# Unsplit 32-bit attention matmuls in place of three-part splits, in a two-layer encoder trunk

## The chip, the core and the metric

The kernel runs on one core of one Trainium2 chip. The metric is the device time of one execution in microseconds (us). The engines are TensorE (PE; its weight loads are listed as PEld), VectorE (DVE), ScalarE (ACT), GpSimd (POOL) and SyncE (SP, which here only issues transfers).

## What is computed

Two layers, each over 512 prompt frames and 32 sample frames, with 1024 features, all in 32-bit floats. A layer is a feed-forward block, a mixer, a second feed-forward block and a gated input embedding, each between two norms. The mixer is where the change lies. From one projection it takes three groups of attention heads, which all have this form, per head and per block of 128 query frames:

```
z = einsum('bqhd,bkhd->bhqk', q, k) * scale       # scores
P = weights(z, mask)                              # 4 heads A: stick-breaking; 8 heads B: softmax; 4 heads C: softmax with a forget bias
o = einsum('bhqk,bkhd->bqhd', P, v)               # value product
```

A and C have 64 features a head in q and k, B has 128 (64 content, 32 rotary, and 32 more that carry the rotation's other half). All have 64 in v. Prompt frames attend causally among themselves (B by chunks of 64); the sample frames attend to a cache of 256 frames and to each other.

## The kernel before

Frames lie in the columns of tiles and features in the 128 partitions. A product in full precision is made of three matmuls: `split` writes a high part (a copy on ACT, rounded to the format that streams in one pass) and a low part (the difference, on DVE), and high x high, high x low and low x high are added up in a bank of PSUM. `gemm` does this for all projections and feed-forward layers.

In the mixer (`mix`), `QK` projects q and k of two heads of A or C at a time (128 features), `VP` their v; `build_q`, `build_k` and `build_v` make those of B from two latents. Each then splits its result. `attend_pair` takes two heads. For each half of the queries (b = 0, 1: 256 frames, of which the first attends to 2 blocks of keys and the second to 4), and each block i of 128 queries in it, it computes the scores of (i + 1) x 128 keys as three matmuls (L405), adds the bias of C (L412) and the mask (L413, an identity in half precision times the mask), makes P in `soft`, transposes P block by block (L135), and splits the transposed P. Then the value product runs over the blocks of keys, three matmuls each (L427 to L429), with the 64 features of v as the weights and 256 queries as columns. Heads of A and C go through this together, those of B one after the other. The sample heads (`attend_sample`) use unsplit 32-bit matmuls throughout.

Banks and tiles limit how far things run ahead: three PSUM banks for scores (`acc`), two for transposes (`tr`), two for projections (`prj`), one for value products (`pv`); two tiles `pa` and four `pb` for the transposed P. The order of the instructions on each engine is made by a scheduler when the program is built, from the order in the source, the dependencies and these limits, so that projections of later heads fill PE between the steps of earlier ones; `hold` keeps a matmul behind the one that was written before it. After the last pair there is little left to fill with.

Of the kernel before, what the change touches and what calls it, by code (L numbers as in the profile page):

```python
# [18 lines left out]
SEQ = 512  # L19
# [16 lines left out]
def trunk(ctx: ExitStack, tc, a, outs, depth=2):  # L36
# [343 lines left out]
    def attend_pair(cb, kind, heads, o, chunk, vget, extra=None):  # L380
# [4 lines left out]
        for b in range(2):  # L385
            cols = slice(b * 256, b * 256 + 256)
            O = tl("pv", [64, 512])
            groups = [[0], [1]] if kind == "B" else [[0, 1]]
            for es in groups:
                pts, lqs = {}, {}  # L390
                for e in es:
                    pts[e] = [tl("pb" if b or (len(es) - 1) * e else "pa", [128, 2 + 2 * b, 256], F32R) for _ in range(2)]
                    for z in pts[e]:
                        nc.gpsimd.memset(f(z[:, 2 * b + 1, 0:128]), 0.0)
                    if extra:
                        lqs[e] = extra(heads[e][0], cols)
                for i in (2 * b, 2 * b + 1):
                    nk, q0 = (i + 1) * 128, i * 128
                    w = max(nk, 256)
                    qs = slice(q0, q0 + 128)  # L400
                    ss = {e: bank("acc") for e in es}
                    for a_, b_ in ((0, 2), (0, 3), (1, 2)):
                        for e in es:
# [4 lines left out]
                    for e in es:  # L408
                        s = ss[e]
                        if extra:  # L410
                            lq, rk = lqs[e]
                            mm(s[:, 0:w], lq[0:100, q0 - b * 256:q0 - b * 256 + 128], rk[0:100, 0:w], start=False, stop=False)  # L412
                        mm(s[:, q0:nk], identb, mask, start=False, stop=True)  # L413
                    for e in es:
                        P = soft(kind, ss[e][:, 0:nk], nk)
                        t = bank("tr")
                        for j in range(i + 1):
                            transpose(t[:, j * 128:j * 128 + 128], P[:, j * 128:j * 128 + 128])
                        qq = slice((i % 2) * 128, (i % 2) * 128 + 128)
                        split(*[z[:, 0:i + 1, qq] for z in pts[e]], t[:, 0:nk].rearrange("p (j s) -> p j s", s=128))  # L420
                for e in es:
                    hd = heads[e][0]
                    ph, pl = pts[e]
                    Oe = O[:, e * 256:e * 256 + 256]
                    for j in range(2 + 2 * b):
                        vh, vl = vget(hd, j)
# [64 lines left out]
    def mix(l, h, x, g_next):  # L491
# [65 lines left out]
        class VP:  # L557
# [25 lines left out]
            def get(s, hd, j):  # L583
                return tuple(z[j // 2][:, j % 2, hd * 64:hd * 64 + 64] for z in (s.vh, s.vl))
# [549 lines left out]
```

## Time and profile before

| | us |
|---|---|
| median of 3 runs | 2480.51 |
| lowest and highest | 2478.15, 2484.81 |
| the profiled execution | 2481.84 |
| its span, first to last instruction | 2480.0 |
| its granted TensorE clock, mean | 0.981 of full speed |

Each layer's attention stands in one stretch: 455 to 691 us in the first layer, 1686 to 1924 us in the second. In the first half of it (A, and the first pair of C) projections are still running, in the second (the last pair of C, B, the sample heads) only the small ones of B. The rest of the span is feed-forward and output layers, in which nothing changes. A stretch's busy times are read against its length; the number of records in it tells how densely an engine was fed.

### The profile page before, as it was taken

The page shows a single profiled execution, that of the slowest core. Times are in us where ns is not written, and L with a number is a line of the kernel's source. Part 1 is how long each engine was busy: PE and PEld are TensorE (multiplying, and loading weights), DVE is VectorE, ACT ScalarE, POOL GpSimd, SP SyncE. Part 2 cuts the span into 40 slices and gives each one's busy share as a digit, 9 for nine tenths or more (in the row PEclk, how much of TensorE's full clock was granted, in tenths as well). Part 3 has the DMA queues.
Part 4 walks back from the last instruction along what each step waited for, and adds up shares of the span by engine and source line. Part 5 has one row for each costly group of instructions (what it writes and reads, how often), then busy time and mean ns, then how long its engine had stood idle before and what let it go on. Part 6 is the DMA issues. An engine that isn't in the chain of part 4 may idle for free.

```text
span 2480.0 us, 45319 instructions
## 1 busy us (share of the span) xinstructions
PE 2390.8 (96%) x18342; PEld 2302.4 (93%) x18342; DVE 1443.3 (58%) x3236; ACT 1083.7 (44%) x2347; POOL 71.7 (3%) x244
## 2 busy tenths in 40 slices
PE   9999999999998999999999999999999989999997
PEld 8999999987788999999999999999876889999997
DVE  6344446777857344446863444477777573444466
ACT  5322224668854322224533222246788543222343
POOL 0000000211000000000000000001110000000000
PEclk9999999999998999999999999999999999999998
DMA  5323322322023323322213323232311233323221
GB/s 161 108 79 90 100 66 82 95 89 55 27 65 115 111 80 90 99 86 86 82 47 98 98 72 106 56 97 91 101 33 34 77 111 98 95 74 102 85 69 37
DMA packets 73600, 207.44 MB, mean 84 GB/s; under 512 B 9312, under 2 KB 18152, under 8 KB 73392
## 3 DMA queue, kind: packets, MB, share of 16 engines
q1 hardware_dynamic: 70288, 195.93, 26.5%
q0 software_dynamic: 3104, 8.62, 1.1%
q8 instruction: 144, 2.36, 0.4%
q14 instruction: 64, 0.52, 0.1%
HBM read 188.21 MB, written 11.85 MB: 81 GB/s over the span
## 4 chain that ended last, share of the span: by engine, by line
PE 88%; DVE 6%; ACT 3%; DMA 2%; issue 1%; SPq 0%; DVEq 0%; ACTq 0%
PE acc L238 12%; PE acc L239 12%; PE acc L240 12%; PE prj L238 10%; PE prj L239 10%; PE prj L240 10%; PE pv L238 4%; PE pv L239 4%; PE pv L240 4%; PE acc L405 2%; PE tr L135 1%; DMA raw<-in_w_ff_gu_dram 1%; DVE z L303 1%; PE pv L427 1%; PE pv L429 1%; PE pv L428 1%
## 5 line engine op out<-in xcount | busy, mean ns | idle before, releaser
L109 ACT ACTIVATE wx<-raw 128x1024 fp32r<-128x1024 f32 (+3 forms) x149 | 139.3, 936 | 269.8 <-PE acc L239 99.4
L109 ACT ACTIVATE wh<-raw 128x1024 fp32r<-128x1024 f32 (+3 forms) x157 | 151.2, 966 | 228.9 <-PE acc L239 101.9
L113 DVE TENSOR_TENSOR wl<-raw,wh 128x1024 fp32r<-128x1024 f32 (+3 forms) x157 | 173.6, 1107 | 80.8 <-ACT wh L109 80.0
L109 ACT ACTIVATE m<-q 128x256 fp32r<-128x256 f32 (+1 forms) x224 | 94.9, 428 | 256.9 <-DVE q L349 251.9
L113 DVE TENSOR_TENSOR wx<-raw,wx 128x1024 fp32r<-128x1024 f32 (+3 forms) x149 | 159.4, 1070 | 77.8 <-ACT wx L109 75.8
L238 PE MATMUL prj<-xa,wh 128*128 128x256 f32 (+3 forms) x632 | 186.4, 295 | 4.6 <-DVE q L346 2.7
L239 PE MATMUL prj<-xb,wh 128*128 128x256 f32 (+3 forms) x632 | 186.2, 295 | 4.5 <-DVE xb L259 4.5
L240 PE MATMUL prj<-xa,wl 128*128 128x256 f32 (+3 forms) x632 | 184.5, 292 | 0.0
L238 PE MATMUL acc<-xa,wx 128*128 128x256 f32 (+1 forms) x600 | 173.9, 290 | 5.4 <-ACT wx L109 5.4
L240 PE MATMUL acc<-xa,wx 128*128 128x256 f32 (+1 forms) x600 | 173.9, 290 | 0.0
L239 PE MATMUL acc<-xb,wx 128*128 128x256 f32 (+1 forms) x600 | 173.6, 289 | 0.0
L239 PE MATMUL acc<-xb,wh 128*128 128x288 f32 (+1 forms) x576 | 166.7, 290 | 0.0
L240 PE MATMUL acc<-xa,wl 128*128 128x288 f32 (+1 forms) x576 | 166.5, 290 | 0.0
L238 PE MATMUL acc<-xa,wh 128*128 128x288 f32 (+1 forms) x576 | 165.6, 290 | 0.0
L240 PE MATMUL prj<-xa,wx 128*128 128x288 f32 (+1 forms) x480 | 139.8, 291 | 1.3 <-DVE wx L113 1.3
L238 PE MATMUL prj<-xa,wx 128*128 128x288 f32 (+1 forms) x480 | 140.4, 293 | 0.0
L239 PE MATMUL prj<-xb,wx 128*128 128x288 f32 (+1 forms) x480 | 140.3, 292 | 0.0
L347 ACT ACTIVATE q<-q 128x256 f32<-128x256 f32 (+1 forms) x176 | 74.3, 425 | 145.6 <-DVE q L346 141.2
L239 PEld LDWEIGHTS prj<-xb,wh 128*128 128x128 f32 (+1 forms) x632 | 119.6, 189 | 7.1 <-DVE xb L259 6.2
L238 PEld LDWEIGHTS prj<-xa,wh 128*128 128x128 f32 (+1 forms) x632 | 119.4, 189 | 7.3 <-DVE q L346 3.2
L240 PE MATMUL acc<-xa,wy 128*128 128x288 f32 (+1 forms) x424 | 123.4, 291 | 0.8 <-DVE wy L113 0.8
L238 PE MATMUL acc<-xa,wy 128*128 128x288 f32 (+1 forms) x424 | 123.7, 292 | 0.4 <-ACT wy L109 0.4
(525 smaller groups left out, 8128.2 us busy)
## 6 DMA issues: line engine op xcount, KB each, us to landing
raw<-in_w_ff_gu_dram SPq DMA_DIRECT2D x174, 512.0 KB, 3.6
raw<-in_w_ff_down_dram SPq DMA_DIRECT2D x64, 384.0 KB, 3.2
raw<-in_w_ff_down_dram SPq DMA_DIRECT2D x64, 320.0 KB, 2.9
raw<-in_w_in_dram SPq DMA_DIRECT2D x22, 512.0 KB, 3.5
raw<-in_w_out_dram SPq DMA_DIRECT2D x16, 512.0 KB, 3.6
raw<-in_w_ple_gate_dram SPq DMA_DIRECT2D x16, 512.0 KB, 3.5
raw<-in_w_v_dram SPq DMA_DIRECT2D x8, 512.0 KB, 3.6
xb<-r SPq DMA_DIRECT2D x32, 128.0 KB, 2.3
```

Of the source, the lines that this page charges most:

```text
L109: act(out, in_, AF.Copy)
L113: tt(lo, src, f(hi), op=ALU.subtract)
L135: nc.tensor.transpose(out, in_, ident[0:n, 0:n])
L238: mm(p, wh[k], xh[k][:, c0:c1], start=i == 0, stop=False)
L239: mm(p, wh[k], xl[k][:, c0:c1], start=False, stop=False)
L240: mm(p, wl[k], xh[k][:, c0:c1], start=False, stop=i == len(ks) - 1)
L303: stt(t, s.y[c][:, c0:c1], s.g[c], s.R[c0], op0=ALU.mult, op1=ALU.mult)
L347: act(g, g, AF.Silu)
L405: one = mm(ss[e][:, 0:w], z[a_][:, qs], z[b_][:, 0:w], start=(a_, b_) == (0, 2), stop=False)
L427: mm(Oe, vh, ph[:, j, :], start=e == 0 and j == 0, stop=False, skip_group_check=True)
L428: mm(Oe, vl, ph[:, j, :], start=False, stop=False, skip_group_check=True)
L429: mm(Oe, vh, pl[:, j, :], start=False, stop=j == 2 * b + 1, skip_group_check=True)
```

## The change

q, k, v and P are no longer split. Scores are one 32-bit matmul a head and block, value products one a head and block of keys. The value products of the two heads of a pair go to the two halves of the partitions of one bank, which are the two halves of the columns of the array. Blocks of P that the mask empties are skipped: the last block of keys is multiplied with 128 queries, not 256, and the first block's scores of A and B are 128 wide, not 256. The transposed P is copied once, by DVE for the first head and by ACT for the second. The heads of B go through as a pair too.

```diff
-            O = tl("pv", [64, 512])
-            groups = [[0], [1]] if kind == "B" else [[0, 1]]
...
-                    pts[e] = [tl("pb" if b or (len(es) - 1) * e else "pa", [128, 2 + 2 * b, 256], F32R) for _ in range(2)]
-                    for z in pts[e]:
-                        nc.gpsimd.memset(f(z[:, 2 * b + 1, 0:128]), 0.0)
...
-                    for a_, b_ in ((0, 2), (0, 3), (1, 2)):
-                        for e in es:
-                            z = heads[e][1]
-                            one = mm(ss[e][:, 0:w], z[a_][:, qs], z[b_][:, 0:w], start=(a_, b_) == (0, 2), stop=False)
-                            if len(es) == 2 and (e, a_, b_) != (0, 0, 2):
-                                hold(one)
...
-                        split(*[z[:, 0:i + 1, qq] for z in pts[e]], t[:, 0:nk].rearrange("p (j s) -> p j s", s=128))
...
-                        mm(Oe, vh, ph[:, j, :], start=e == 0 and j == 0, stop=False, skip_group_check=True)
-                        mm(Oe, vl, ph[:, j, :], start=False, stop=False, skip_group_check=True)
-                        mm(Oe, vh, pl[:, j, :], start=False, stop=j == 2 * b + 1, skip_group_check=True)
-                    (copy if e else nc.vector.tensor_copy)(o[chunk][64 * e:64 * e + 64, cols], Oe)
+            O = tl("pv", [128, 256])
+            pts = [tl("pb" if b else "pa", [128, 2 + 2 * b, 256]) for _ in heads]
+            lqs = [extra(hd, cols) for hd, _ in heads] if extra else None
+            for i in (2 * b, 2 * b + 1):
+                nk, q0 = (i + 1) * 128, i * 128
+                w = max(nk, 256) if extra else nk
+                ss = [bank("acc") for _ in heads]
+                for e, (_, (q, k)) in enumerate(heads):
+                    one = mm(ss[e][:, 0:w], q[:, q0:q0 + 128], k[:, 0:w], start=True, stop=False)
+                    if e and kind != "B":
+                        hold(one)
+                for e, s in enumerate(ss):
                     if extra:
...
+                    mm(s[:, q0:nk], identb, mask, start=False, stop=True)
+                    P = soft(kind, s[:, 0:nk], nk)
+                    t = bank("tr")
...
+                    (copy if e else nc.vector.tensor_copy)(pts[e][:, 0:i + 1, qq],
+                                                           t[:, 0:nk].rearrange("p (j s) -> p j s", s=128))
+            end = 2 * b + 1
+            for j in range(end + 1):
+                qs = slice(128 if j == end else 0, 256)
+                for e, (hd, _) in enumerate(heads):
+                    one = mm(O[64 * e:64 * e + 64, qs], vget(hd, j), pts[e][:, j, qs], start=j == 0, stop=j == end,
+                             skip_group_check=True)
+                    if j or e:
+                        hold(one)
+            (copy if b else nc.vector.tensor_copy)(o[chunk][:, cols], O)
...
-                split(s.hi[:, c0:c0 + 256], s.lo[:, c0:c0 + 256], s.kf[:, c0:c0 + 256])
...
-                    split(s.vh[t // 2][:, t % 2, :], s.vl[t // 2][:, t % 2, :], vf)
...
-        for r in (0, 64):
-            nc.sync.dma_start(out=f(krt[r + 32:r + 64, 0:SEQ]), in_=f(krt[r:r + 32, 0:SEQ]))
...
+                vb.append(tl("xa", [128, 512]) if t < 4 else tl("h", [DEC, 512]))
+                (nc.vector.tensor_copy if t % 2 else copy)(vb[t], p)
...
+                for r in (64, 96):
+                    nc.sync.dma_start(out=k[r:r + 32, 0:SEQ], in_=kl[0:32, 0:SEQ])
...
-                    split(kh[0:64, c0:c0 + 256], kl_[0:64, c0:c0 + 256], p[64 * e:64 * e + 64, 0:256])
+                    (nc.vector.tensor_copy if e else copy)(tiles[e][0:64, c0:c0 + 256], p[64 * e:64 * e + 64, 0:256])
...
-                    split(*[z[:, c0:c0 + 256] for z in tiles[e]], t[:, 0:256])
```

How the built programs differ, at three places. The first is PE at the first pair of group A in layer 0: `acc` are the banks of the two heads' scores, `m` the tiles of q and k, `cb` the mask and its identity, L238 to L240 a projection that fills in. Before (L405 scores, L413 mask):

```order
L405 MATMUL acc_723_5192<-m_665_4812,m_654_4764 128x256
L405 MATMUL acc_722_5191<-m_666_4813,m_654_4764 128x256
L405 MATMUL acc_723_5192<-m_666_4813,m_654_4764 128x256
L405 MATMUL acc_722_5191<-m_665_4812,m_655_4765 128x256
L405 MATMUL acc_723_5192<-m_665_4812,m_655_4765 128x256
L413 LDWEIGHTS cb_714_5176
L413 MATMUL acc_722_5191<-cb_714_5176 128x128
L413 LDWEIGHTS cb_714_5176
L413 MATMUL acc_723_5192<-cb_714_5176 128x128
```

And now (L395 scores, L402 mask):

```order
L395 MATMUL acc_710_5159<-m_663_4808,m_654_4764 128x128
L402 LDWEIGHTS cb_704_5150
L402 MATMUL acc_710_5159<-cb_704_5150 128x128
L395 MATMUL acc_711_5160<-m_663_4808,m_654_4764 128x128
L402 LDWEIGHTS cb_704_5150
L402 MATMUL acc_711_5160<-cb_704_5150 128x128
```

The scores of the two heads stood together, with both masks behind them; now the first head's mask stands between them. Over the whole program the two scores of a pair of A or C follow each other directly at 4 places of 32.

The second place is PE at a second half (b = 1) of the third pair of B in layer 0: `pv` is the bank of the value products, `pb` the transposed P, `xa` the values, the other rows are sample heads. Before (head 0 of the pair only):

```order
L427 MATMUL pv_1289_7934<-pb_1290_7935,xa_983_6763 64x256
L428 MATMUL pv_1289_7934<-pb_1290_7935,xa_984_6764 64x256
L405 MATMUL acc_1390_8262<-xb_1227_7701,m_1233_7727 128x512
L405 MATMUL acc_1390_8262<-xb_1228_7702,m_1233_7727 128x512
L405 MATMUL acc_1390_8262<-xb_1227_7701,m_1234_7728 128x512
L413 LDWEIGHTS cb_714_5176
L413 MATMUL acc_1390_8262<-cb_714_5176 128x128
L135 MATMUL tr_1308_8005<-cst_66,t_1305_7998 128x128 x3
L429 MATMUL pv_1289_7934<-pb_1291_7936,xa_983_6763 64x256
L427 MATMUL pv_1289_7934<-pb_1290_7935,xa_986_6771 64x256
```

And now (L414, both heads, `pb_1124` and `pb_1125`):

```order
L414 MATMUL pv_1123_7104<-pb_1124_7105,xa_942_6494 64x256
L444 MATMUL acc_1165_7269<-h_1164_7265,s_649_4756 32x288
L196 MATMUL prj_1236_7472<-r_1221_7438,cst_66 128x288
L414 MATMUL pv_1123_7104<-pb_1125_7106,xa_942_6494 64x256
L414 MATMUL pv_1123_7104<-pb_1124_7105,xa_944_6500 64x256
L414 MATMUL pv_1123_7104<-pb_1125_7106,xa_944_6500 64x256
L414 MATMUL pv_1123_7104<-pb_1124_7105,xa_946_6506 64x256
L414 MATMUL pv_1123_7104<-pb_1125_7106,xa_946_6506 64x256
L414 MATMUL pv_1123_7104<-pb_1124_7105,xa_948_6512 64x128
L414 MATMUL pv_1123_7104<-pb_1125_7106,xa_948_6512 64x128
```

The first product of head 0 goes ahead by itself and the other seven follow in one run, alternating between the heads. In the program, 30 value products stand alone, and the others in 16 runs of seven, 14 of three and 2 of four.

The third place is DVE at about the same point: `tr` is the bank of the transposed P, `col` the maxima and sums of the softmax. Before:

```order
L113 TENSOR_TENSOR pb_1291_7936<-tr_1296_7951,pb_1290_7935 128x3x128
L444 TENSOR_REDUCE col_1379_8221<-acc_1377_8215 128x1
L446 RECIPROCAL col_1368_8178<-col_1368_8178 128x1
L113 TENSOR_TENSOR pb_1291_7936<-tr_1301_7969,pb_1290_7935 128x4x128
L446 RECIPROCAL col_1375_8206<-col_1375_8206 128x1
```

And now:

```order
L408 COPY pb_1124_7105<-tr_1131_7119 128x3x128
L434 RECIPROCAL col_1144_7158<-col_1144_7158 128x1
L839 COPY h_1161_7253<-r_1041_6842 64x256
L840 COPY h_1161_7253<-s_649_4756 128x32
```

The subtraction that read the high part from ACT is gone; DVE copies the first head's P, and ACT alone the second head's. Over both layers 184 instructions fewer stand on ACT and 184 on DVE.

## Rows read from the trace of the kernel before

**Rows 1.** The page: each engine's busy time, share and instructions.

```profile
PE 2390.8 (96%) x18342; PEld 2302.4 (93%) x18342; DVE 1443.3 (58%) x3236; ACT 1083.7 (44%) x2347; POOL 71.7 (3%) x244
```

**Rows 2.** Busy time of each engine by stretch, with its records.

```profile
core 0: us, PE busy (x) PEld busy (x) DVE busy (x) ACT busy (x) POOL busy (x), PEclk, DMA share, GB/s
440.00:500.00 60.00, 60.00 (x461) 55.81 (x460) 46.25 (x99) 37.78 (x93) 12.07 (x37) 1.00 0.29 90
...
560.00:691.00 131.00, 121.95 (x809) 93.61 (x809) 102.31 (x300) 110.72 (x321) 10.95 (x48) 1.00 0.15 43
...
1790.00:1924.00 134.00, 124.30 (x812) 95.23 (x811) 100.92 (x299) 110.37 (x320) 10.73 (x49) 0.97 0.14 38
```

**Rows 3.** Timeline of PE, a projection before value products: start, length, weights, columns.

```profile
603.98 0.28 PE L789 MATMUL prj<-m,wl 128*128 128x256 f32 x1
604.10 0.28 PE L427 MATMUL pv<-pb,h 128*64 128x256 f32 x1
604.21 0.28 PE L428 MATMUL pv<-pb,h 128*64 128x256 f32 x1
```

**Rows 4.** Timeline of PE, sample heads' unsplit value product; and its durations by line.

```profile
1809.98 1.02 PE L478 MATMUL tr<-y,t 128*128 128x256 f32 x4
...
L478 PE MATMUL tr<-y,t x20: 374/379/483, 1810.0 to 1920.7; 128*128 128x256 f32 x16, 32*128 32x256 f32 x4
```

**Rows 5.** Timeline of PE, the sample heads' bias of C, in four column groups.

```profile
593.88 0.69 PE L463 MATMUL acc<-st 36*32 36x288 f32 x8
594.50 0.33 PE L427 MATMUL pv<-pb,h 128*64 128x256 f32 x1
```

**Rows 6.** Timeline of PE, split scores of B and the mask matmuls behind them.

```profile
622.77 0.69 PE L405 MATMUL acc<-xb,m 128*128 128x384 f32 x3
623.30 0.23 PE L413 MATMUL acc<-cb 128*128 128x128 bf16 x1
...
623.94 0.86 PE L405 MATMUL acc<-xb,m 128*128 128x512 f32 x3
624.63 0.23 PE L413 MATMUL acc<-cb 128*128 128x128 bf16 x1
```

**Rows 7.** Timeline of PE, split scores of two heads of A or C, 64 rows each.

```profile
483.42 0.96 PE L405 MATMUL acc<-m,m 64*128 64x512 f32 x5
484.31 0.28 PE L413 MATMUL acc<-cb 128*128 128x128 bf16 x2
...
497.78 0.62 PE L405 MATMUL acc<-m,m 64*128 64x256 f32 x5
498.33 0.28 PE L413 MATMUL acc<-cb 128*128 128x128 bf16 x2
...
520.94 0.76 PE L405 MATMUL acc<-m,m 64*128 64x384 f32 x5 [0.38 <-DVE t L440]
521.63 0.29 PE L413 MATMUL acc<-cb 128*128 128x128 bf16 x2
```

**Rows 8.** ACT's groups by shape, 560 to 691 us: busy, mean ns, idle before.

```profile
L109 ACT ACTIVATE m<-q 128x256 fp32r<-128x256 f32 x20 | 8.2, 414 | 1.3 <-DVE q L843 1.3
L109 ACT ACTIVATE pb<-tr 128x512 fp32r<-128x512 f32 x12 | 7.1, 594 | 5.2 <-PE tr L135 5.0
L109 ACT ACTIVATE pb<-tr 128x384 fp32r<-128x384 f32 x12 | 5.9, 493 | 0.4 <-PE tr L135 0.4
L109 ACT ACTIVATE xb<-prj 64x256 fp32r<-64x256 f32 x16 | 5.7, 377 | 1.0 <-PE prj L789 0.7
L109 ACT ACTIVATE pa<-tr 128x256 fp32r<-128x256 f32 x10 | 3.8, 381 | 1.3 <-PE tr L135 1.2
L109 ACT ACTIVATE pa<-tr 128x128 fp32r<-128x128 f32 x9 | 2.4, 269 | 0.7 <-PE tr L135 0.6
```

**Rows 9.** Waits, POOL's clearing of P: waited for, us, times, longest.

```profile
POOL pb L394 <- PE pv L428: 98.9, 20, 9.5
```

**Rows 10.** The page's transfers: the key's rotary part into B's tiles.

```profile
xb<-r SPq DMA_DIRECT2D x32, 128.0 KB, 2.3
```

More of the change, by code (lines that the diff above doesn't have):

```diff
@@ new lines, in attend_pair @@
+            O = tl("pv", [128, 256])
[10 more added lines that the diff above has]
+                for e, s in enumerate(ss):
+                    if extra:
+                        lq, rk = lqs[e]
+                        mm(s[:, 0:w], lq[0:100, q0 - b * 256:q0 - b * 256 + 128], rk[0:100, 0:w], start=False, stop=False)
+                    mm(s[:, q0:nk], identb, mask, start=False, stop=True)
+                    P = soft(kind, s[:, 0:nk], nk)
+                    t = bank("tr")
+                    for j in range(i + 1):
+                        transpose(t[:, j * 128:j * 128 + 128], P[:, j * 128:j * 128 + 128])
+                    qq = slice((i % 2) * 128, (i % 2) * 128 + 128)
+                    (copy if e else nc.vector.tensor_copy)(pts[e][:, 0:i + 1, qq],
+                                                           t[:, 0:nk].rearrange("p (j s) -> p j s", s=128))
@@ L536, in half @@
                     s.w = proj(s.col0)
-                    s.hi, s.lo = unit("m", F32R), unit("m", F32R)
-                    s.kf = unit("kf")
+                    s.kf = unit("m")
                 n = c1 - c0
@@ L564, in tile @@
                     s.wh, s.wl = ([z[i][:, k, :] for z in w for k in range(4)] for i in range(2))
-                    s.vh, s.vl = ([tl(s.tag, [128, 2, 256], F32R) for _ in range(2)] for i in range(2))
+                    s.v = [tl(s.tag, [128, 2, 256]) for _ in range(2)]
                 n = 128 if t < 4 else DEC
@@ L583, in get @@
             def get(s, hd, j):
-                return tuple(z[j // 2][:, j % 2, hd * 64:hd * 64 + 64] for z in (s.vh, s.vl))
+                return s.v[j // 2][:, j % 2, hd * 64:hd * 64 + 64]
         def attend_qk(kind, js, c, chunk, v, extra=None):
@@ L590, in attend_qk @@
                 r = slice(e * 64, e * 64 + 64)
-                heads.append((2 * c + e, tuple(z[r, 0:SEQ] for z in (q.hi, q.lo, k.hi, k.lo))))
+                heads.append((2 * c + e, tuple(z.kf[r, 0:SEQ] for z in (q, k))))
             attend_pair(cb, kind, heads, o, chunk, v.get, extra)
@@ L677, in mix @@
             tt(kl[0:32, c0:c1], kl[0:32, c0:c1], u[0:32, :], op=ALU.add)
-            split(krh[:, c0:c0 + 256], krl[:, c0:c0 + 256], kl[0:32, c0:c0 + 256])
             fx, e = t[64:68, :], u[64:68, :]
@@ L815, in build_k @@
         def build_k(hp):
-            tiles = [tuple(unit("xb", F32R) for _ in range(2)) for _ in range(2)]
-            for kh, kl_ in tiles:
-                nc.sync.dma_start(out=f(kh[64:128, 0:SEQ]), in_=f(krt[0:64, 0:SEQ]))
-                nc.sync.dma_start(out=f(kl_[64:128, 0:SEQ]), in_=f(krt[64:128, 0:SEQ]))
+            tiles = [unit("xb") for _ in range(2)]
+            for k in tiles:
+                for r in (64, 96):
+                    nc.sync.dma_start(out=k[r:r + 32, 0:SEQ], in_=kl[0:32, 0:SEQ])
             for c0, c1 in HALVES:
@@ L833, in build_q @@
             wh, wl = uq
-            tiles = [tuple(unit("m", F32R) for _ in range(2)) for _ in range(2)]
+            tiles = [unit("m") for _ in range(2)]
             for c0, c1 in HALVES:
@@ L871, in attend_b @@
         def attend_b(hp, q, k):
-            heads = [(2 * hp + e, tuple(z[:, 0:SEQ] for z in (*q[e], *k[e]))) for e in range(2)]
-            attend_pair(cb, "B", heads, o, 2 + hp, lambda hd, j: tuple(z[:, hd * 64:hd * 64 + 64] for z in vb[j]))
+            heads = [(2 * hp + e, (q[e][:, 0:SEQ], k[e][:, 0:SEQ])) for e in range(2)]
+            attend_pair(cb, "B", heads, o, 2 + hp, lambda hd, j: vb[j][:, hd * 64:hd * 64 + 64])
         uq = [load_uq(0), None]
```

41 lines of the change are left out of this document (2 added, 39 removed).

## The prediction

> **What bounds the kernel now.** I read the page's totals first [rows 1]: TensorE (PE) is busy for 96% of the span, so the first guess is that only matmul time counts. Busy time hides waits, though, because records overlap, so I then cut the span into stretches [rows 2]. The column to read is PEld, the weight loads, one per matmul. Where attention of group A hides behind projections (440 to 500 us), it is 93% busy. In the second half of each mixer (560 to 691 and 1790 to 1924 us: group B, the last pair of group C, the sample heads) it is only 71%, with fewer matmuls per microsecond. At those 93%, 93.6 us of loads would fill 101 us, so about 30 us per layer are stalls. In the same rows ScalarE (ACT) is busy 110.7 of 131 us and VectorE (DVE) 102.3. There the softmax chain and the split copies queue on ACT and DVE, and PE waits. So the change has to be priced twice: as PE work everywhere in attention, and as ACT and DVE work in these two stretches, 265 us together.
>
> **Units.** A split product is three matmuls, each streaming its columns once. Ordinary ones of 256 columns follow each other every 0.12 us, value products (64 weight columns) every 0.115 us [rows 3]. An unsplit 32-bit matmul also exists in this trace: the sample heads' value product issues two matmuls over full rows, and the trace holds four records, 1.02 us in all, the last 0.38 us long [rows 4]. Three steps in 0.64 us are 0.214 us a record, two records an instruction: 0.43 us for 256 columns. I scale with the columns: 0.21 us for 128, 0.64 for 384 and 0.86 for 512. So one unsplit matmul costs four units where the split costs three.
>
> **Scores of group B.** Split, a head pays 0.36 us for each of its two 256-wide tiles (three matmuls at 0.12), 0.53 for 384 and 0.69 for 512 columns, from the first score to the mask matmul behind it [rows 6]: 1.94 us. Unsplit, with the first tile now 128 wide, it pays 0.21 + 0.43 + 0.64 + 0.86 = 2.14. Sixteen heads in two layers, 0.20 each: **+3.2 us**.
>
> **Scores of groups A and C.** Their heads take 64 rows each, and before, six matmuls of two heads stand together, so the heads share the array: a pair of tiles costs 0.55, 0.69 and 0.89 us for 256, 384 and 512 columns up to the mask [rows 7] (the trace holds five of the six records there), hardly more than one head alone. The excess over one head, 0.16 to 0.20 us, is the cost of entering and leaving the 64-row shape; I use 0.19. A pair of heads costs 2 x 0.55 + 0.69 + 0.89 = 2.68 us, eight pairs 21.4. In the changed order the mask matmul of the first head stands between the two scores in 28 of 32 places (the first order piece shows it). It uses all rows, so the scores can't overlap. A head of A then pays 2.14 + 4 x 0.19 = 2.90, one of C, whose first tile stays 256 wide, 3.12; eight of each make 48.2. The four places where two scores still touch give back a score and a shape change each, 2 x 0.40 + 2 x 0.62 = 2.0. Sum, 48.2 - 21.4 - 2.0: **+24.8 us**. If the shape change is paid once a pair after all, 32 x 0.19 = 6.1 less: +18.7.
>
> **Value products.** Before: 576 matmuls at 0.115 us are 66.2 us. After: 192, of which 64 are 128 wide. Do two heads run side by side when they share the rows and differ in the columns? No row has 128 x 64 tiles of 32 bits. The nearest is the sample heads' bias product [rows 5]: eight records in four column groups of the same rows, 288 columns each, and the next matmul starts 0.62 us after the first. One behind the other, at 0.214 us for 256 columns and so 0.24 for 288, they would need 1.9 us; so columns do share. In the changed order the first product of head 0 mostly stands alone and the other three or seven in one run (second order piece). With pairs inside a run overlapped, a short block (b = 0) costs 0.43 + 0.43 + 0.21 and a long one (b = 1) 0.43 + 3 x 0.43 + 0.21: 3.00 us for two heads, 48.0 for sixteen pairs: **-18.2 us**. Bounds: nothing overlaps, 128 x 0.43 + 64 x 0.21 = 68.5, +2.3; all overlaps, 16 x (4 x 0.43 + 2 x 0.21), -32.0.
>
> PE work alone thus rises by about 10 us.
>
> **ACT and DVE.** In one late stretch, ACT loses five of ten copies of P per width (0.59 + 0.49 + 0.38 + 0.27 us, times five: 8.7), the 16 high parts of q (0.414 each: 6.6), 8 of 16 copies of k (3.0), two of four copies of v (1.2, at P's 0.59 for 512 columns) and half of ten output copies (1.9, at k's 0.377 for 64 x 256): 21.4 us of 110.7 [rows 2, 8]. DVE loses every subtraction and takes the other half of the copies; at the same widths that is about 23 us of 102.3 (third order piece). What returns lies between nothing, if the stalls are the latency of one chain, and all 21.4 a layer, if ACT is the bound; the 30 us of stalls lie above both. I take half, 10.7 a layer, since ACT at 85% is near its limit but its queue is not always full: **-21.4 us**. In the first half of the mixers, PE is fed without gaps [rows 2], and I count nothing.
>
> **The rest.** POOL's 128 clearings of the upper triangle go. POOL waited on PE there [rows 9], so they end no wait of PE themselves, and I count nothing. These waits also say that the P tiles of one head were reused only after its value product; now each head has its own, which supports a return on ACT. The key's four doubling transfers go, and build_k's 32 transfers carry half the bytes; all run ahead of use under other heads' work. If that cover were gone it would be a wait of some 2.3 us, what such a transfer takes to land [rows 10].
>
> **Sum.** +3.2 + 24.8 - 18.2 - 21.4 = -11.6 us. The profiled execution took 2481.8 us (span 2480.0), 1.3 above the median of 2480.5. That gives **2470 us**.
>
> **Rivals.**
> 1. *ACT is the true bound of the late stretches*: all 42.8 us return, +9.8 - 42.8 = -33.0, **2449 us**. For it: ACT idles only 20 of 131 us. Against it: PE busy reads 93% there too, and its own work stays.
> 2. *The late stretches are one chain's latency* (score, maximum, exponential, scale, transpose, copy): nothing returns, and the 9.8 us of PE work stay, **2492 us, slower**. For it: value products now wait for both heads, and the unsplit score itself is 0.2 us longer in the chain at 512 columns. It decides as soon as less than 9.8 us come back in two layers.
> 3. *The columns don't run side by side*: value products +2.3 instead of -18.2, **2491 us, slower**. The row in four column groups speaks against it, but it has fewer rows.
> 4. *Entering the two-column shape empties the array as the 64-row shape does*: 62 separate runs of value products at 0.19 us are +11.8, **2482 us**. Today's value products also use 64 columns and follow full-width matmuls with no gap: 0.12 us from L789 to L427 [rows 3]. The Trainium skill has this as a rule (TensorEngine Tiling (Array Packing), section Key Properties): changing the tiling mode, not just the tile, drains the engine. By the rule this rival holds; by the row at 603.98 it is free, at least in the first column group.
>
> **Chances.** The forecast 0.40 (its own range 2462 to 2480), rival 1 0.17, rival 2 0.22, rival 3 0.13, rival 4 0.08. Within 0.3%, about 7.4 us either way and the least that this measurement tells from no change, I put a fifth of the forecast, half of rival 4 and a fifth of rivals 2 and 3: 0.08 + 0.04 + 0.07 = 0.19. Faster: the rest of the forecast, rival 1 and a quarter of rival 4, 0.32 + 0.17 + 0.02 = 0.51. Slower: 0.28 + 0.02 = 0.30. For 8 in 10 the range must reach to rival 1 and past rivals 2 and 3 with the bounds of the scores: 2446 to 2500.
>
> **What would show it.** Value products: records of two heads starting within some 10 ns of each other inside a run. Scores of A and C: single, with a mask matmul between them, and 48 us in place of 21. ACT busy near 90 us in the late stretch and that stretch shorter by some 10 us per layer, while the stretch of group A grows by 4 to 8. I am wrong if the late stretch keeps its length, if head 1's value product starts only when head 0's ends, or if a new wait, for the third score bank or for head 1's P, takes the place of the splits.

## The result, and the profile after

The changed kernel takes 2454.24 us (median; 2452.86 to 2457.55) against 2481.66 for the kernel before on the same chip: ratio 0.9888, interval 0.9876 to 0.9900, or **27.4 us faster**. The sign was right and the range held it, but 11.6 us were forecast.

The page's totals answer to [rows 1]; ACT lost 58 us, DVE 64:

```profile
PE 2382.6 (97%) x18022; PEld 2253.3 (92%) x18022; DVE 1379.4 (56%) x3052; ACT 1025.6 (42%) x2163; POOL 48.8 (2%) x116
```

Busy time by stretch, for [rows 2]:

```profile
core 0: us, PE busy (x) PEld busy (x) DVE busy (x) ACT busy (x) POOL busy (x), PEclk, DMA share, GB/s
440.00:500.00 60.00, 60.00 (x428) 52.78 (x427) 41.14 (x84) 32.28 (x74) 10.59 (x29) 0.98 0.26 86
...
560.00:691.00 131.00, 125.44 (x763) 85.66 (x762) 91.30 (x268) 96.11 (x275) 3.45 (x6) 0.99 0.15 45
...
1790.00:1924.00 134.00, 128.44 (x804) 91.83 (x802) 92.01 (x266) 96.61 (x274) 1.06 (x2) 0.99 0.14 42
```

From 560 to 691 us ACT and DVE are both less busy (96 for 111, 91 for 102 us) and PE more (125 for 122). A window of fixed times shows little else, since its content has shifted. By content, from the first matmul of B's v to the last value product, the late stretch takes 105.7 us in each layer, for 128.8 and 135.6 before: 23 and 30 less, where some 10 a layer were forecast. What lies ahead of it in the mixer grew by 6 and 12 us.

The timeline of PE in the second half of a mixer, for [rows 3, 6]: value products of two heads (L414), scores of B (L395), masks (L402).

```profile
start us, us, engine line op out<-in xcount [idle before <-releaser]
...
620.90 1.08 PE L395 MATMUL acc<-xb,m 128*128 128x512 f32 x2
621.82 0.22 PE L402 MATMUL acc<-cb 128*128 128x128 bf16 x1
621.97 0.65 PE L414 MATMUL pv<-pb,xa 128*64 128x256 f32 x2
622.54 0.33 PE L135 MATMUL tr<-cst,t 128*128 128x128 f32 x1
...
624.08 0.29 PE L240 MATMUL prj<-m,wl 128*128 128x288 f32 x1
624.30 1.73 PE L414 MATMUL pv<-pb,xa 128*64 128x256 f32 x14
625.96 0.55 PE L135 MATMUL tr<-cst,t 128*128 128x128 f32 x3
626.34 1.02 PE L395 MATMUL acc<-xb,m 128*128 128x512 f32 x2
627.20 0.22 PE L402 MATMUL acc<-cb 128*128 128x128 bf16 x1
```

The scores of 512 columns cost 0.92 and 0.86 us to their masks; 0.86 was worked out from [rows 4]. The seven value products (14 records) from 624.30 to 625.96 cost 1.66 us. One behind the other they would need 7 x 0.43 less 0.43 for the two halves, 2.6 us; with pairs side by side 1.50. So the columns are shared. But the run starts 0.22 us after the last projection, not 0.13, and costs 0.16 more than 1.50; a lone product costs 0.57, not 0.43. Unsplit value products are paid for at their entry and their exit.

The same for scores of A (64 rows each), for [rows 7]:

```profile
463.52 0.70 PE L395 MATMUL acc<-m,m 64*128 64x256 f32 x2
464.15 0.23 PE L402 MATMUL acc<-cb 128*128 128x128 bf16 x1
...
471.25 1.12 PE L395 MATMUL acc<-m,m 64*128 64x512 f32 x2
472.31 0.23 PE L402 MATMUL acc<-cb 128*128 128x128 bf16 x1
```

They stand alone, 0.63 and 1.06 us to the mask: 0.43 and 0.86 with 0.20 for the shape, as forecast (0.19).

ACT's groups from 560 to 691 us, for [rows 8]:

```profile
L109 ACT ACTIVATE pb<-tr 128x512 f32<-128x512 f32 x6 | 3.6, 597 | 3.2 <-PE tr L135 3.1
L109 ACT ACTIVATE xb<-prj 64x256 f32<-64x256 f32 x8 | 3.0, 371 | 2.8 <-PE prj L769 2.8
```

Half of the copies are left, at the same length. POOL's waits [rows 9] are gone with its clearings, and no wait on the key's transfers [rows 10] has come.

**A balance of the mixers.** Busy times overlap, so I summed the time from each matmul's start to the next one's, by the kind of the first, from the first v projection of a mixer to its last value product, both layers together. A wait is then counted with the matmul ahead of it. All sums below are worked out from the matmul records of the profiled executions and hold to about 1 us; "value" has the 48 records of the sample heads in it (some 13 us).

```
us            total  score  value   mask  transp   bias  projections and rest
before        551.3   70.6   91.9   12.8    55.0    8.7   312.4
after         526.4   83.3   68.9    9.4    47.1    8.2   309.4
relief        511.9   70.7   82.4    8.5    42.5    8.3   299.5
load_all      575.0   87.9   73.6    9.3    58.7    8.5   337.1
one_half      545.3   84.3   89.9    8.6    44.1    8.3   310.1
adjacent      545.5   69.2   66.5   27.2    52.6   10.2   319.8
mixed         508.5   69.9   67.2    9.3    45.2    8.3   308.7
load_dve      565.1   84.5   71.1   11.1    59.7    8.2   330.5
load_dve_sb   530.0   83.3   66.4    9.7    45.3    8.5   316.9
```

From before to after it gives 24.9 of the 27.4 us: scores +12.7, value products -23.0, everything else -14.6. The scores were to cost +28.0.

### The profile page after: what moved, and what is told of

Same layout as the page of the kernel before. It is cut to its first block, busy times and chain, and to the rows that moved or that the text cites. A ratio compares the mean times of both kernels' runs of the same rounds, so it can differ in the third digit from the quotient of the medians.

```text
span 2451.1 us, 43918 instructions
## 1 busy us (share of the span) xinstructions
PE 2382.6 (97%) x18022; PEld 2253.3 (92%) x18022; DVE 1379.4 (56%) x3052; ACT 1025.6 (42%) x2163; POOL 48.8 (2%) x116
## 4 chain that ended last, share of the span: by engine, by line
PE 92%; DVE 4%; DMA 2%; ACT 1%; issue 0%; SPq 0%; DVEq 0%; ACTq 0%
PE acc L238 12%; PE acc L239 12%; PE acc L240 12%; PE prj L238 10%; PE prj L239 10%; PE prj L240 10%; PE pv L238 4%; PE pv L239 4%; PE pv L240 4%; PE acc L395 3%; PE pv L414 2%; PE tr L135 2%; DMA raw<-in_w_ff_gu_dram 1%; DVE z L303 1%; PE prj L556 1%; PE prj L557 1%
## 5 line engine op out<-in xcount | busy, mean ns | idle before, releaser
L238 PE MATMUL prj<-xa,wh 128*128 128x256 f32 (+3 forms) x632 | 187.8, 297 | 4.6 <-DVE q L346 2.7
L109 ACT ACTIVATE m<-q 128x256 fp32r<-128x256 f32 (+1 forms) x192 | 81.9, 431 | 255.0 <-DVE q L349 252.7
L240 PE MATMUL prj<-xa,wl 128*128 128x256 f32 (+3 forms) x632 | 184.3, 292 | 0.0
L238 PE MATMUL acc<-xa,wx 128*128 128x256 f32 (+1 forms) x600 | 174.4, 291 | 5.7 <-ACT wx L109 5.7
L240 PE MATMUL acc<-xa,wx 128*128 128x256 f32 (+1 forms) x600 | 173.4, 289 | 0.0
L240 PE MATMUL acc<-xa,wl 128*128 128x288 f32 (+1 forms) x576 | 166.8, 290 | 0.0
L238 PE MATMUL acc<-xa,wh 128*128 128x288 f32 (+1 forms) x576 | 166.6, 292 | 0.0
L240 PE MATMUL prj<-xa,wx 128*128 128x288 f32 (+1 forms) x480 | 139.5, 291 | 1.3 <-DVE wx L113 1.3
L238 PE MATMUL prj<-xa,wx 128*128 128x288 f32 (+1 forms) x480 | 140.6, 293 | 0.0
L238 PEld LDWEIGHTS prj<-xa,wh 128*128 128x128 f32 (+1 forms) x632 | 120.1, 190 | 7.7 <-DVE q L346 3.2
L240 PE MATMUL acc<-xa,wy 128*128 128x288 f32 (+1 forms) x424 | 122.7, 289 | 0.7 <-DVE wy L113 0.7
L238 PE MATMUL acc<-xa,wy 128*128 128x288 f32 (+1 forms) x424 | 123.3, 291 | 0.0
```

The lines of the kernel that those rows point to most:

```text
L109: act(out, in_, AF.Copy)
L238: mm(p, wh[k], xh[k][:, c0:c1], start=i == 0, stop=False)
L240: mm(p, wl[k], xh[k][:, c0:c1], start=False, stop=i == len(ks) - 1)
```

## The experiments

Chips differ by some 3 us, so the runs are compared by their ratio to the kernel before on the same chip; 0.001 is 2.5 us, and the changed kernel stands at 0.9888. An instruction's place in its engine's row is made anew in each kernel by the scheduler.

### What the dropped split work is worth

**relief** is the kernel before with all its matmuls, but without the work that splits: one rounded copy of q, k, v and P stands for both parts, so the low parts are left out of the result.

```diff
-                        split(*[z[:, 0:i + 1, qq] for z in pts[e]], t[:, 0:nk].rearrange("p (j s) -> p j s", s=128))
+                        (copy if e else nc.vector.tensor_copy)(pts[e][0][:, 0:i + 1, qq], t[:, 0:nk].rearrange("p (j s) -> p j s", s=128))
...
-                    split(kh[0:64, c0:c0 + 256], kl_[0:64, c0:c0 + 256], p[64 * e:64 * e + 64, 0:256])
+                    (nc.vector.tensor_copy if e else copy)(kh[0:64, c0:c0 + 256], p[64 * e:64 * e + 64, 0:256])
```

> The kernel before with its own matmuls (three per product, row sharing in A and C, 64 columns in the value products), but without the splits: the low part is the high part itself, so ACT and DVE do only what the changed kernel has them do. The low parts are left out of the result. Theory A (the gain is the ACT and DVE time taken out of the attention stretches; PE work rose by some 25 us): 2425 to 2440 us, faster than the changed kernel. Rival B (the gain is PE's, from the value products that share the columns, and ACT and DVE relief is worth little): 2470 to 2482 us.

Measured: 2441.01 us, 0.9837 (0.9820 to 0.9853), 40 us faster than before, 1 us above theory A's range. One rounded copy in place of two parts also frees half of the tiles of P, q, k and v and half of POOL's clearings, so this run alone does not tell the engines' work from the tiles.

**load_all** is the changed kernel with the dropped work back on ACT and DVE, the differences written into a spare tile (one of the two `kf` tiles goes for it, here and in every run with subtractions).

```diff
-                    (copy if e else nc.vector.tensor_copy)(pts[e][:, 0:i + 1, qq], ...)
+                    copy(dst, src)
+                    tt(tl("sl", [128, 512])[:, 0:nk].rearrange("p (j s) -> p j s", s=128), src, dst, op=ALU.subtract)
```

> The changed kernel with the split work put back on ACT and DVE and nothing changed on PE: every P, q, k and v is copied by ACT and subtracted by DVE into a spare tile that nobody reads. Theory A: 45 to 55 us come back, 2495 to 2510 us. Rival B: at most 8 us, 2454 to 2462 us.

Measured: 2501.61, 1.0083 (1.0068 to 1.0098), 48 slower than the changed kernel, as theory A has it, with the tiles of q, k, v and P as they are. Both ways, the relief is worth 40 to 48 us, twice the 21.4 of the forecast. The matmuls themselves then cost: after against relief +13, load_all against before +21.

### Which matmuls

**scores_only**: the kernel before with unsplit scores; P, v and the value products stay split.

```diff
-                    for a_, b_ in ((0, 2), (0, 3), (1, 2)):
-                        for e in es:
...
+                    for e in es:
+                        q, k = heads[e][1]
+                        one = mm(ss[e][:, 0:w], q[:, qs], k[:, 0:w], start=True, stop=False)
```

> The kernel before with the scores alone changed: q and k unsplit, one 32-bit matmul a score; P, v and the value products split as before. PE pays some 30 us more (A and C no longer share rows), ACT is relieved of some 34 us. Theory A: 2475 to 2492 us, no gain. Rival B: 2505 to 2515 us, the whole PE price.

Measured: 2470.55, 0.9951 (0.9933 to 0.9968): 12 faster than before, where no gain or a loss was expected. In its balance the scores cost 13.9 us more than before and all the rest 26 less.

**pv_only**: the other half; the changed kernel with q, k and the scores split again.

> The changed kernel with the scores alone split again: q and k high and low, three matmuls with row sharing as before; P and v unsplit, value products side by side in the columns. PE pays some 5 us less than before, ACT is relieved of some 43 us. Theory A: 2435 to 2452 us. Rival B, in which the columns' sharing is the gain: 2452 to 2462 us.

Measured: 2456.96, 0.9901 (0.9879 to 0.9923), as the changed kernel, in rival B's range and above theory A's. So once P and v are unsplit, unsplitting the scores costs on PE about what it saves elsewhere.

**one_half**: the changed kernel with both heads' value products in the first 64 columns, so that they can't share.

```diff
-            O = tl("pv", [128, 256])
+            O = tl("pv", [64, 512])
```

> The changed kernel with both heads' value products in the first 64 columns of the array, one after the other, and two output copies. By the changed kernel's trace a run of seven costs 1.66 us with sharing and would cost 2.6 without: some 16 us of PE work more. Theory A: 2464 to 2474 us, still faster than before. Rival B: the whole gain goes, 2478 to 2484 us.

Measured: 2474.01, 0.9972 (0.9961 to 0.9983), 21 slower than the changed kernel; the balance shows all of it at the value products (89.9 for 68.9). Sharing the columns is real and worth 21 us. What entry and exit cost is there as well, although only the first 64 columns are used. A lone product and a run of seven:

```profile
486.94 0.65 PE L414 MATMUL pv<-pb,y 128*64 128x256 f32 x2
487.51 0.39 PE L238 MATMUL prj<-xa,wh 128*128 128x256 f32 x1
...
489.76 2.81 PE L414 MATMUL pv<-pb,y 128*64 128x256 f32 x14
492.50 0.40 PE L240 MATMUL prj<-xa,wl 128*128 128x288 f32 x1
```

They cost 0.57 us for 0.43 and 2.74 for 2.58. So this price is not that of using both halves.

**adjacent**: the changed kernel with the two scores of A and C and the value products of a block held together in program order.

```diff
-                    if e and kind != "B":
+                    if kind != "B":
                         hold(one)
...
-                    if j or e:
-                        hold(one)
+                    hold(one)
```

> The changed kernel with both scores of a pair of A or C kept in order, so that 26 of 32 pairs of scores stand together, before their masks, and not 4. Each pair that overlaps saves one score and one change of shape, 0.4 to 1.05 us by the changed kernel's trace, some 20 us of PE work. If PE work counts in full: 2432 to 2440 us. If the stretches of A and C have slack: 2446 to 2454 us.

Measured: 2482.06, 1.0001 (0.9988 to 1.0015), 28 **slower** than the changed kernel, a miss. The scores did fall, by 14 us in the balance, but masks, transposes and projections took 34 more. One line of PE's waits, 544 to 692 us (waited for, us, times, longest), which the changed kernel does not have, shows where:

```profile
PE tr L135 <- ACT t L434: 10.3, 6, 4.0
```

Projections had moved ahead: from 410 to 560 us stand 930 matmuls other than scores, masks, transposes of P and value products, 843 in the changed kernel. Fewer are left to fill PE between a head's mask and its transposes, and PE waits out the softmax. **adj_pv**, with the second of the two edits alone, tells which hold did it.

> The changed kernel with the first value product of each block also held to the one ahead of it in the program, as in the run with both holds; the scores of A and C are left as changed. That run was 28 slower than the changed kernel: its scores fell from 83 to 69 us and its value products from 69 to 67, but mask matmuls, transposes and fillers took 34 us more to what follows them, since fillers had moved ahead of the late stretch. Theory A (the holds on the scores moved the fillers): this one stays at 2448 to 2456. Rival B (the holds on the value products did, since the first product of a block waits for both heads' P): 2470 to 2485.

Measured: 2453.33, 0.9888 (0.9872 to 0.9905): nothing. It was the holds on the scores, alone or together with the others.

### Where the relief acts

Four runs put parts of load_all's work back into the changed kernel: **load_p** that of P, **load_qkv** that of q, k and v, **load_ac** that of groups A and C, **load_b** that of B (`if kind == "B":` around the lines above, and so on).

> The changed kernel with the split work of P alone put back on ACT and DVE (ACT copies both heads' P, DVE subtracts into a spare tile). P's copies are some 28 us of ACT's time and 31 us of DVE's in two layers. Theory A with the late stretch bound by ACT: 15 to 30 us come back, 2469 to 2484 us. Rival B: 2454 to 2458 us.

Measured: 2465.43, 0.9931 (0.9915 to 0.9947), +11, between the two ranges.

> The changed kernel with the split work of q, k and v alone put back: ACT copies each once more, in place, DVE subtracts into a spare tile. Some 45 us of ACT's time in two layers, about half of it in the first half of the mixers, where projections cover it. Theory A: 10 to 25 us come back, 2464 to 2479 us. If all the relief that matters is in P: 2454 to 2459 us.

Measured: 2463.20, 0.9919 (0.9901 to 0.9937), +8, again between them.

> The changed kernel with the dropped copies and subtractions of groups A and C alone put back on ACT and DVE, into a spare tile (their P, q, k and v). With those of all groups it took 2501.6, 47 more than the changed kernel. Theory A (the prediction's step that the first half of the mixers hides this work, so that only group B's part costs): 2454 to 2464. Rival B (the work costs alike wherever it stands, about half of the 47): 2470 to 2485.

Measured: 2461.14, 0.9916 (0.9897 to 0.9934), +7.

> The changed kernel with the dropped copies and subtractions of group B alone put back (its P, q, k and v), into a spare tile. Theory A (only the late stretches pay, and group B stands there): 30 to 47 more than the changed kernel, 2484 to 2501. Rival B (alike everywhere): 2470 to 2485. Theory C (the cost appears only when the load of all groups is there together, as P alone and q, k, v alone cost 11 and 9): 2460 to 2470.

Measured: 2483.28, 1.0009 (1.0000 to 1.0019), +30, the low edge of theory A; rival B's range reaches there too, but load_ac rules it out. So the place was right: B's work in the late stretch costs four times what that of A and C does. But the price is not a sum by kind of work: P alone and q, k, v alone make some 18 of 48.

### Which engine, or which bank

**load_act** puts back ACT's copies alone, **load_dve** DVE's subtractions alone.

```diff
+                    dst, src = pts[e][:, 0:i + 1, qq], t[:, 0:nk].rearrange("p (j s) -> p j s", s=128)
-                    (copy if e else nc.vector.tensor_copy)(pts[e][:, 0:i + 1, qq], ...)
+                    copy(dst, src)                                                            # load_act
+                    (copy if e else nc.vector.tensor_copy)(dst, src)                          # load_dve
+                    tt(tl("sl", [128, 512])[:, 0:nk].rearrange(...), src, dst, op=ALU.subtract)  # load_dve
```

> The changed kernel with ACT's dropped copies alone put back, of all groups (all copies of P, k and v on ACT, q, k and v copied once more), with no subtraction; DVE has less to do than in the changed kernel. Copies and subtractions together cost 47. Theory A (ACT's queue ends the waits of the late stretches, as rival 1 of the prediction has it): 25 to 45 more than the changed kernel, 2479 to 2499. Rival B (DVE's does, or the chain through the subtraction): 0 to 10, 2454 to 2464.

Measured: 2453.48, 0.9880 (0.9857 to 0.9902): nothing.

> The changed kernel with DVE's dropped subtractions alone put back, of all groups, into a spare tile; the copies stay shared between ACT and DVE, so DVE has some more to do than in the kernel before. Theory A (ACT is the bound): 0 to 15, 2454 to 2469. Rival B (DVE is): 25 to 50, 2479 to 2504. Theory C (either engine alone is hidden, and only both together cost): both runs within 10 of the changed kernel.

Measured: 2495.08, 1.0046 (1.0032 to 1.0061), +39.

ACT, on which the forecast of the relief was built, does not bound the stretch. Its copies do count beside the subtractions: load_all, with both, is 9 us slower than load_dve. DVE's own busy time does not either: **load_dve_sb** has the same subtractions, but those of P and of B's k and v read the copy in SBUF, not the bank in PSUM.

```diff
-                    tt(tl("sl", [128, 512])[:, 0:nk].rearrange("p (j s) -> p j s", s=128), src, dst, op=ALU.subtract)
+                    tt(tl("sl", [128, 512])[:, 0:nk].rearrange("p (j s) -> p j s", s=128), dst, dst, op=ALU.subtract)
```

> As the run with DVE's subtractions alone, but those of P, B's k and B's v read only tiles in SBUF, so that no PSUM bank is kept longer; as many instructions of the same shapes. Theory A (the queue of DVE is what costs): 2485 to 2500, as with the subtractions that read PSUM. Rival B (the bank of the transposes, held until the subtraction has read it, is what costs): 2454 to 2470.

Measured: 2460.94, 0.9915 (0.9898 to 0.9931), +7. Busy time from 562 to 690 us, first load_act:

```profile
562.00:690.00 128.00, 122.89 (x746) 83.86 (x745) 76.51 (x230) 108.22 (x318) 3.45 (x6) 0.97 0.16 46
```

then load_dve:

```profile
562.00:690.00 128.00, 113.89 (x662) 72.06 (x661) 109.85 (x311) 86.76 (x245) 3.47 (x6) 1.00 0.13 40
```

and load_dve_sb:

```profile
562.00:690.00 128.00, 120.06 (x714) 80.67 (x713) 116.89 (x340) 92.42 (x262) 3.44 (x6) 0.97 0.17 50
```

With ACT at 108 us of 128 PE keeps 746 matmuls; with DVE at 117, 714; with DVE at 110 but the banks held, 662. By content, as above, the late stretch takes 104 us a layer in load_act, 107 and 111 in load_dve_sb, 121 and 133 in load_dve. The subtraction is no longer from PSUM (load_dve, groups by shape on DVE from 560 to 691 us) than from SBUF (load_dve_sb):

```profile
L410 DVE TENSOR_TENSOR sl<-tr,pb 128x512 f32<-128x512 f32 x12 | 8.2, 686 | 1.4 <-ACT pb L109 1.1
```

```profile
L410 DVE TENSOR_TENSOR sl<-pb 128x512 f32<-128x512 f32 x12 | 8.2, 683 | 1.7 <-ACT pb L109 1.6
```

What differs is who waits. PE's waits on subtractions in load_dve, 544 to 692 us:

```profile
PE tr L135 <- DVE sl L410: 2.9, 6, 1.2
...
PE prj L238 <- DVE sl L808: 0.7, 1, 0.7
```

and its weight loads':

```profile
PEld tr L135 <- DVE sl L410: 2.5, 4, 1.4
...
PEld prj L238 <- DVE sl L808: 1.0, 1, 1.0
```

In load_dve_sb none of these lines is left. There are two banks for the transposes and two for projections; a bank of P is held for a copy and a subtraction (0.59 and 0.69 us for 512 columns) and for what DVE does in between, where the changed kernel holds it for the copy alone. **load_dve_tr** lets only P's subtractions read PSUM, **load_dve_prj** only those of B's k and v.

> DVE's subtractions put back as before, but only those of P read PSUM; B's k and v are subtracted from tiles in SBUF. Theory A (the two banks of the transposes): 2485 to 2497, nearly all of the 34 between the runs with all from PSUM and none. Rival B (the two banks of the projections): 2458 to 2466. Theory C (each adds its part): 2468 to 2482.

Measured: 2472.97, 0.9972 (0.9957 to 0.9986), +21, as theory C has it.

> DVE's subtractions put back as before, but only those of B's k and v read PSUM; those of P read tiles in SBUF. Theory A (the banks of the transposes): 2458 to 2466. Rival B (the banks of the projections): 2485 to 2497. Theory C (each adds its part): 2468 to 2482.

Measured: 2491.96, 1.0035 (1.0025 to 1.0045), +36, as rival B has it. Over load_dve_sb's 7 that is 14 for the transposes' banks, some 30 for the projections', and 32 for both: each alone costs, the projections' most, and they don't add.

The longest wait in load_dve_prj shows how, DVE first, then PE, then the stretch behind it:

```profile
633.99 1.54 DVE L410 TENSOR_TENSOR sl<-pa 128x128 f32<-128x128 f32 x4
635.57 2.60 DVE L410 TENSOR_TENSOR sl<-pb 128x384 f32<-128x384 f32 x4
638.27 0.42 DVE L808 TENSOR_TENSOR sl<-prj,xb 64x256 f32<-64x256 f32 x1
638.70 0.43 DVE L807 COPY xb<-prj 64x256 f32<-64x256 f32 x1
639.16 0.95 DVE L808 TENSOR_TENSOR sl<-prj,xb 64x256 f32<-64x256 f32 x2
```

```profile
639.73 0.55 PE L238 MATMUL prj<-m,wh 128*128 128x256 f32 x1 [5.52 <-DVE sl L808]
640.08 0.41 PE L239 MATMUL prj<-m,wh 128*128 128x256 f32 x1
640.30 0.41 PE L240 MATMUL prj<-m,wl 128*128 128x256 f32 x1
```

```profile
635.50:645.70 10.20, 5.79 (x24) 5.52 (x25) 7.74 (x18) 0.38 (x2) 0.00 (x0) 0.50 0.00 0
```

Eight subtractions of P, for which nobody waits, stand in DVE's row ahead of those that hold the banks of B's k (L808). PE idles for 5.5 us, and its granted clock falls to half, the 1.2 GHz level, so that the matmuls behind the wait follow each other every 0.21 us, not 0.12. The second layer has the same wait and the same fall. Together they make 11 us of waiting and, at 24 matmuls a layer and some 0.1 us each, an estimated 5 us of slow matmuls: about half of the 30.

So the price takes both: a bank held for a second reader, and a long row ahead of that reader. load_dve_sb has the row without the held banks and costs 7. load_p and load_qkv, whose copies stand on ACT, hold the same two kinds of banks with a shorter row: load_p costs 11 for load_dve_tr's 21, load_qkv 8 for load_dve_prj's 36.

### A version that beats both

**mixed** is the changed kernel with the scores of A and C split and row-shared as before, those of B unsplit; q and k of A and C are split again.

```diff
+                turns = [(e, x) for x in ((0, 2), (0, 3), (1, 2)) for e in range(2)]
+                if kind == "B":
+                    turns = [(e, (0, 1)) for e in range(2)]
...
+                split(s.hi[:, c0:c0 + 256], s.lo[:, c0:c0 + 256], s.kf[:, c0:c0 + 256])
```

> The changed kernel with the scores of groups A and C split again (q and k in two parts, two heads sharing the rows of the array); B's scores, P, v and the value products stay as changed. From the two traces, scores of A and C take 34 us to the next matmul when split and 47 us unsplit, those of B the same either way (36 and 37). Theory A (matmul time counts in full where A and C run, because fillers stand there, and the ACT and DVE work of the split of their q and k is mostly hidden behind projections): 12 us less than the changed kernel or a little under, 2442 to 2449. Rival B (the split work on ACT and DVE costs as much as the scores save, as in the run with all scores split again): 2453 to 2459.

Measured: 2437.05, 0.9819 (0.9803 to 0.9834): 17 faster than the changed kernel, 45 than the kernel before, and below both ranges. In the balance the scores fall from 83.3 to 69.9, all the rest by 4, and nothing rises by more than 0.1: those splits read SBUF and stand under projections.

**mixed_act** has in addition all copies of P and of B's k and v on ACT.

> The version with scores of A and C split and B's unsplit (2437), with all copies of P, of B's k and of B's v on ACT instead of half of them on DVE: DVE loses some 32 us of work in both layers, ACT gains about as much. Theory A (DVE's queue bounds the late stretches, ACT has room): 0 to 15 less, 2422 to 2437. Rival B (the two are balanced, or the chain's latency bounds): 2437 to 2455.

Measured: 2437.24, 0.9816 (0.9801 to 0.9831): no difference, where the two ranges meet; which engine copies does not matter here.

## Why the prediction was right in sign and too small

**Scores of B** (+3.2): from the records, 36.1 us to the next matmul before and 36.7 after, +0.6. Right to 2.6 us.

**Scores of A and C** (+24.8): the first step that failed, a term that was mis-sized. They went from 34.5 to 46.6 us, +12.1. The price after was right (48.2 less 2.0 forecast); that of before was not 21.4. I read the x5 in [rows 7] as six records with one lost. None is lost, as the first order piece, with five rows of L405, already shows: in 30 of the 32 places the first of the six stands elsewhere by itself, and pays the shape once more. These 30 cost 11.7 us to the next matmul, all others 22.8. PE's timeline of the kernel before has it, 6.5 us ahead of the five at 497.78:

```profile
491.06 0.27 PE L240 MATMUL prj<-xa,wl 128*128 128x256 f32 x1
491.26 0.38 PE L405 MATMUL acc<-m,m 64*128 64x256 f32 x1
491.57 0.40 PE L238 MATMUL prj<-xa,wh 128*128 128x288 f32 x1
```

From 491.06 to 491.57 are 0.51 us, for 0.24 of two matmuls in a row. It fits that scores_only gained: its scores cost 13.9 us more than before, not 28.

**Value products** (-18.2): 78.9 us before with the waits inside, 56.6 after, -22.3, and some 0.09 us more ahead of each of 62 runs, 5.6 us (behind a mask or a transpose it is 0.11 and 0.17, so a little more): -16.7. That the sum came out right is luck, since its parts did not (66.2 and 48.0 forecast): by the balance 9.5 of the 22.3 go in relief too, where the matmuls are as before. Rival 3 is refuted by one_half. Rival 4's mechanism is real: 8.6 above 48.0 inside the runs and 5.6 at their entries, 14 us for 62 runs, 0.23 each. By the rule of the Trainium skill that the prediction set beside it (TensorEngine Tiling (Array Packing), section Key Properties), that a change of the tiling mode drains the engine, the trace agrees in these 0.23 us. But the two halves are not the cause, since one_half pays the same in one; it is the unsplit product of 64 weight columns, to which the row of a split one at 603.98 did not carry over.

**ACT and DVE** (-21.4): the second step that failed. "I take half, 10.7 a layer, since ACT at 85% is near its limit" gave the wrong size from the wrong engine. Alone the relief measured 40 us, put back 48, and ACT's copies by themselves cost nothing. What returns is for the most part time for which PSUM banks wait for a second reader on DVE: 32 of the 39 us that the subtractions cost go when they read SBUF. Rival 1 has the nearest number (2449) and the wrong mechanism; rival 2 fails, since far more than 9.8 us came back. The Trainium skill has the form of such a shortage of banks (Perfetto Trace Analysis, section Optimization Strategy): the same gap, repeating on the engine that should be full, can mean that there isn't enough SBUF or PSUM for the next tile. Here the trace agrees: six waits of 2.9 us in all for the transposes' banks in load_dve, and the 5.5 us of both layers in load_dve_prj.

**The clock**, for which the prediction has no term. In the profiled execution before, it stood at half, the 1.2 GHz level, at three places inside the mixers, 17 us in all; PE had waited ahead of them. The first, with the stretch ahead of it:

```profile
520.60:524.00 3.40, 2.17 (x11) 1.10 (x11) 2.59 (x7) 2.86 (x7) 0.00 (x0) 1.00 0.00 0
524.00:530.80 6.80, 5.51 (x24) 4.61 (x25) 5.36 (x12) 5.61 (x17) 1.90 (x6) 0.50 0.07 25
```

69 matmuls stand in the three; at some 0.1 us each that is an estimate of 7 us. From 442 us on, the changed kernel's first mixer has no such place, nor has its second from 1660 us on, and relief has none either. So part of what fewer waits gave came through the clock; no run separates it. In adjacent the clock stood at half for 34 us inside the mixers.

The first half of the mixers was counted as nothing; load_ac, which has the last pair of C in it too, puts it at some 7 us or less.

**The sum.** Relief -39.4 in the balance (before to relief), scores +12.6, value products -13.5 (relief to after), and +15.4 that no term had, at masks, transposes and projections: entries, 5.6, and the rest perhaps waits of the longer scores and of value products for both heads, which no run separates. Together -24.9 in the mixers. The two errors both made the forecast gain too small: the relief was 18 too small, the scores' price 15 too large, and of these 33 the unforeseen 15 and the value products' 5 took back 20.

**What stays open.** The waits that name a subtraction sum to about 7 us in load_dve's stretch, PE and weight loads together, against the 16 a layer that reading from SBUF saves. Between load_dve and load_dve_sb 658 of the 18022 records of PE's order differ by line and tile, so part of the price may come through the order that the scheduler makes when banks come free later; how much was not separated. Another share of the eight banks was not tried.

## To carry to other kernels

Where a result is evicted from PSUM in two passes, ask how long its bank is held, what stands ahead of the second reader in its engine's row and who needs the next bank, before counting the engines' busy time: subtractions as second readers cost 39 us here, the same work from SBUF 7. Count the groups of a row-shared form over the whole trace before pricing one from its best example, since a member that stands alone pays the entry again. Splitting a change by stage can beat it: where projections cover the split work and two heads share rows, keep the split; where the work feeds from PSUM, drop it.

## What the runs showed of the hardware

Two heads' 32-bit value products in the two column halves started 5 to 8 ns apart inside a run and shared the time. Entering and leaving unsplit products of 64 columns cost about 0.23 us a run, in one half (one_half) or in both, although split products in 64 columns [rows 3] paid nothing. Behind a wait of 5.5 us PE's granted clock stood at half for 10.2 us, and matmuls of 256 columns followed each other every 0.21 us for 0.12 (load_dve_prj). An unsplit 32-bit matmul took 0.43 us for 256 columns in every shape measured, 3.6 times the 0.12 of one step of the split.
